# Loads of the normed activations h issued from ScalarE's queue instead of SP's

## Chip, cores and metric

The kernel runs on one core of a Trainium2 chip, in one launch. The metric is the device time of that launch in microseconds. Three runs of the kernel before gave 2426.85 us as median (2415.17 to 2428.43); one more execution was profiled.

## What is computed

One layer of a streaming encoder, for 2048 frames of a new stream (16 tiles of 128 rows) and for 8 running streams of 16 frames each (one more tile, called NT). The part that the change touches is the input projection:

```python
h = rms_norm(x, norm_g) * (1 + scale) + shift
qa, ka, va, za, qb, kb, vb, zb, ga, gb = split(h @ w_in)
```

`h` is (2176, 1024), `w_in` is (1024, 6144). Branch a is a differential softmax attention with rotated q and k (4 heads), branch b a stick-breaking attention (8 heads); each is gated with silu(z), goes through a matrix of its own, is weighted with sigmoid(g), and the sum goes through `w_out`, a residual and a last norm. Rotated keys and values are outputs too.

## The kernel before

Products need float32 accuracy, so each operand is kept as two float16 halves, high and low, and each product is three matmuls (high x high, high x low, low x high).

**Stage 1** (to about 140 us) makes h. It is written to DRAM, transposed and halved, as `hT_d`, one group of four tiles at a time (L1070). For the first unit h is still in the SBUF (`at_hand`).

**Stage 2** is one long interleaved stretch. There are 8 *units* u: four pairs of a head of branch a (`kind` 0) with two heads of branch b (`kind` 1). Within each unit the 17 tiles are worked off, NT first, then 0 to 15. `steps` lists the 136 pairs (u, t). For each:

- `fetch_h` (L400 to L403) loads h of the tile from `hT_d` into one of three SBUF buffers `hs`, taken in turn: 512 KB, one DMA on SP's queue. The buffer of load n is that of load n - 3.
- `project` (L405) gives 24 products of 512 columns (`mm`, L423 to L426: 8 pieces of the depth, three each) into a PSUM bank of the tag `mm`. `finish` then evacuates q, k, v and z (L440, L289, L452; for branch a the rotation on POOL, L459 to L464) and issues the stores (L474, L475, L477).
- `gate_piece` (L486 to L497) gives 24 products of 256 columns (512 in the last unit, none in the first) with the same h into the single bank of the tag `t`, evacuates them on ScalarE with L496, and stores them with L497. These are the last readers of the buffer.
- `transpose_qk` (L501) turns q and k on TensorE; `scores` (L614) gives the score products (L628 to L632), evacuated by L547 on VectorE (branch a) or as sigmoids by L119 on ScalarE (branch b), with the scan L605 behind them. Weights are split in halves (L289, L561, L562) and transposed by a DMA on SP's queue into `wt` (`turn`, L569); two steps later `pv` multiplies them with v (L676 to L681).

`line` (L839 to L869) is the list of the projection pieces of all steps in order, 12 pieces of two products each and then the gate pieces. At piece `H_AT` = 2 of step m it fetches h of step m + 1 (L855). For each step the main loop (L1202) takes as many pieces as are due and interleaves them with the score chunks and the value products by cost (`interleave`, L91). Preparation of the next unit's weights and norms of later operands (L828, one 512 KB load each) are spread between them.

That is the order in which the program is written. The framework then schedules it: it takes the instructions by their dependencies and by a modelled time, sets each into the queue of its engine, and adds the semaphore waits. An engine's queue is worked off in order. `tc.add_manual_dep` with `NOSYNC` adds an edge for the scheduler alone, without a semaphore; `act` (L117) uses it to keep the activations in order of writing. Each DMA counts up one of eight completion counters, given out in turn, and waits for the DMA that had its counter before.

**Stage 3** (from about 1797 us) applies the gates, the branch matrices and `w_out`, with the attention of the running streams beside it.

The functions that the change touches, and what calls them:

Of the kernel before, what the change touches and what calls it, by code (L numbers as in the profile page):

```python
# [23 lines left out]
NOSYNC = mybir.DependencyInfo(mybir.DependencyClass.NoSync, mybir.DependencyReason.DATA)  # L24
# [3 lines left out]
KT = D // P  # L28
# [81 lines left out]
def layer_kernel(ctx: ExitStack, tc: tile.TileContext, a: dict):  # L110
    nc = tc.nc
    V, S, G, T = nc.vector, nc.scalar, nc.gpsimd, nc.tensor
    load = nc.sync.dma_start
# [3 lines left out]
    def act(**kw):  # L117

        i = S.activation(**kw)  # L119
        if last_table[0] is not None:  # L120
            tc.add_manual_dep(i.ins, last_table[0].ins.name, NOSYNC, reason="table order")
        last_table[0] = i
        return i

    x_p = a["x_prompt"][0]
    x_s = a["x_sample"].rearrange("b s d -> (b s) d")
# [35 lines left out]
    hT_d = [dram.tile([P, w // P, 2, KT, P], F16, name=f"hT_d{g}") for g, (_, w) in enumerate(GROUPS)]  # L162
# [235 lines left out]
    at_hand, ahead, fetched = {}, {}, []  # L398

    def fetch_h(u, t):  # L400
        ahead[u, t] = hs[len(fetched) % 3].bitcast(F16).rearrange("p (f k n) -> p f k n", f=2, n=P)
        fetched.append(t)
        load(out=ahead[u, t], in_=hT_d[t // 4][:, t % 4, :, :, :])  # L403

    def project(U, t):  # L405

        kind, h, sc, sq = U["kind"], U["h"], U["sc"], U["sq"]
        g, i = t // 4, t % 4
        box = {}

        def start():
            if t in at_hand:
                box["h"] = at_hand.pop(t)
            else:
                if (U["u"], t) not in ahead:
                    fetch_h(U["u"], t)
                box["h"] = ahead.pop((U["u"], t))
            box["p"] = bank("mm")
            if kind == 0:
                box["r"] = stg.tile([P, 96], F32, tag="rope", name="rope")  # L420
                load(out=box["r"], in_=a["shapes"][:, t * 96 : t * 96 + 96])

        def mm(n):  # L423
            hi, wi = ((0, 0), (0, 1), (1, 0))[n % 3]
            k = n // 3
            T.matmul(box["p"], box["h"][:, hi, k, :], U["w"][k][:, wi, :], start=(n == 0), stop=(n == 3 * KT - 1))  # L426

        def piece(n):
            if n == 0:
                start()  # L430
            for j in range(2 * n, 2 * n + 2):
                mm(j)
            if n == 11:
                finish()
# [103 lines left out]
    def evacuate(job, seg, c, p, lo, n, sc_pos, sc_neg, ch):  # L538

        buffers(job, seg)  # L540
        if job["U"]["kind"] == 0:
            if "mx" not in job:
                job["mx"] = tiny.tile([P, 2, 4], F32, tag="mx", name="mx")
                job["nch"] = 0
            job["nch"] = max(job["nch"], ch + 1)
            dst = seg[("p", "n")[c]]
            V.tensor_scalar(out=dst[:, lo : lo + n], in0=p[:, 0:n], scalar1=sc_pos, scalar2=None,  # L547
                            op0=ALU.mult, op1=ALU.max, accum_out=job["mx"][:, c, ch : ch + 1])
        else:

            act(out=seg["p"][:, lo : lo + n], in_=p[:, 0:n], func=AF.Sigmoid, scale=sc_pos)
            act(out=p[:, 0:n], in_=p[:, 0:n], func=AF.Sigmoid, scale=sc_neg)
# [18 lines left out]
    def softmax_pair(job):  # L571

        segs = job["segs"]
        nm = tiny.tile([P, 2], F32, tag="nm", name="nm")
        V.tensor_reduce(out=nm, in_=job["mx"][:, :, 0 : job["nch"]], axis=AX.X, op=ALU.max, negate=True)
        l = tiny.tile([P, 2, 2], F32, tag="l", name="l")
        for i, seg in enumerate(segs):
            nk = (seg["hi"] - seg["lo"]) * P
            for c in range(2):
                w = seg[("p", "n")[c]][:, 0:nk]  # L580
                act(out=w, in_=w, func=AF.Exp, bias=nm[:, c : c + 1], accum_out=l[:, c, i : i + 1])
        r = tiny.tile([P, 3], F32, tag="r", name="r")
        sums = l[:, :, 0]
        if len(segs) > 1:
            V.tensor_tensor(out=sums, in0=l[:, :, 0], in1=l[:, :, 1], op=ALU.add)
        V.reciprocal(out=r[:, 0:2], in_=sums)
        V.scalar_tensor_tensor(out=r[:, 2:3], in0=sums[:, 0:1], scalar=r[:, 1:2], in1=nlam, op0=ALU.mult, op1=ALU.mult)
        V.tensor_tensor(out=r[:, 0:1], in0=r[:, 0:1], in1=ls[:, 0:1], op=ALU.mult)
        for seg in segs:
            nk = (seg["hi"] - seg["lo"]) * P  # L590
            p, n = seg["p"][:, 0:nk], seg["n"][:, 0:nk]
            V.scalar_tensor_tensor(out=p, in0=n, scalar=r[:, 2:3], in1=p, op0=ALU.mult, op1=ALU.add)
            turn(job, seg, r[:, 0:1])
# [253 lines left out]
    def projection(m):  # L847
        u, t = steps[m]
        made = []

        def piece(i):
            if i == 0:
                begin(u, t)
                made.extend(project(units[u], t))
            if i == H_AT and not at_hand and m + 1 < len(steps):  # L855
                fetch_h(*steps[m + 1])
            made[i]()

        return [lambda i=i: piece(i) for i in range(12 + 3 * GATES[u][1] // 128)]
# [342 lines left out]
    for n in range(len(steps) + PV_LAG):  # L1202
        made, qk, vs = [], [], []
        if n < len(steps):
            u, t = steps[n]
# [182 lines left out]
```

## Time and profile before

| | |
|---|---|
| three runs, median (lowest to highest) | 2426.85 us (2415.17 to 2428.43) |
| the profiled execution | 2416.58 us, span 2414.4 us |
| mean granted TensorE clock | 0.954 |
| stretch in which the loads of h are issued | 140 to 1797 us |
| DMAs on the one hardware queue | 75.3% of the DMA engines' time |

An engine's busy time leaves out the issuing of DMAs. In rows of waits, the line named waited for what stands behind the arrow: microseconds in total, how often, the longest. In the timeline a row is start, duration, engine, line, operation, tiles, count and, in brackets, how long the engine was idle just before. PEld is the weight load of TensorE, which runs ahead of the matmuls (PE): a stall for h shows first at PEld. SPq is SP's queue of DMA issues; ACTq is what ScalarE's sequencer does itself. Lines are those of the kernel before.

### The profile page before, as it was taken

What the parts mean: (1) busy time and instruction counts of PE and PEld (TensorE: products, weight loads), DVE (VectorE), ACT (ScalarE), POOL (GpSimd) and SP (SyncE); (2) the same over time, 40 slices, a digit from 0 to 9 for tenths busy, and PEclk for the clock granted to TensorE, in tenths of its full rate; (3) what the DMA queues carried; (4) which work ended last, traced back from release to release, by engine and by line L of the source; (5) the groups of instructions that cost most, each with busy time, mean ns of one, the idle gap of its engine ahead of it and who ended that gap; (6) DMA issues with size and microseconds to landing.
All of it is one profiled execution on the core that took longest, in us unless ns stands there. A gap on an engine that the chain in (4) does not pass through costs nothing. (4 is left out here: it accounts for less than half of the span.)

```text
span 2414.4 us, 45136 instructions
## 1 busy us (share of the span) xinstructions
PE 2129.1 (88%) x16366; PEld 1247.2 (52%) x16366; DVE 1746.9 (72%) x3668; ACT 1664.5 (69%) x3264; POOL 754.2 (31%) x607
## 2 busy tenths in 40 slices
PE   5879998899999899899988898999995688888998
PEld 2435665565665556556555555655553344444443
DVE  4868778886676788667778976657778767777754
ACT  3658788886777878566777876665777667666652
POOL 1733023453102346220124542102334333332322
PEclk7989999999999999999999999999997889999999
DMA  9668969985886998577588866756688999998521
GB/s 334 215 204 205 215 161 217 221 182 134 189 219 168 211 195 177 129 174 177 134 215 175 182 154 149 186 129 158 154 179 184 274 240 254 252 244 214 158 104 53
DMA packets 854000, 453.91 MB, mean 188 GB/s; under 512 B 539050, under 2 KB 806362, under 8 KB 853264
## 3 DMA queue, kind: packets, MB, share of 16 engines
q1 hardware_dynamic: 853776, 451.03, 75.3%
q8 instruction: 128, 2.10, 0.4%
q14 instruction: 96, 0.79, 0.1%
HBM read 249.80 MB, written 73.44 MB: 134 GB/s over the span
## 5 line engine op out<-in xcount | busy, mean ns | idle before, releaser
L611 POOL TENSOR_TENSOR sc_p<-sc_p,sc_n 128x127 f32<-128x127 f32 (+7 forms) x192 | 318.9, 1664 | 755.4 <-DVE sc_n L605 736.6
L426 PEld LDWEIGHTS <-hs 128*128 128x128 f16 x3120 | 278.9, 99 | 320.5 <-DMA hs<-hT_d 58.4
L426 PE MATMUL ps_mm<-wa,hs 128*128 128x512 f16 x1590 | 405.9, 388 | 28.3 <-DMA hs<-hT_d 28.3
L426 PE MATMUL ps_mm<-wb,hs 128*128 128x512 f16 x1530 | 391.2, 385 | 22.6 <-DMA hs<-hT_d 19.1
L493 PEld LDWEIGHTS <-hs 128*128 128x128 f16 x2856 | 275.5, 98 | 93.9 <-DVE qst L521 4.3
L605 DVE TENSOR_TENSOR_SCAN sc_n<-ps_s,sc_n,zero_t 128x512 f32<-128x512 f32 x192 | 245.6, 1279 | 48.6 <-ACT ps_s L119 42.4
L562 DVE TENSOR_TENSOR sc_n<-sc_p,sc_n 128x128 f16<-128x128 f32 (+7 forms) x192 | 232.1, 1214 | 27.8 <-ACT sc_n L561 27.3
L628 PE MATMUL ps_s<-k,qst 128*128 128x512 f16 (+3 forms) x640 | 224.8, 352 | 29.0 <-DVE sc_n L605 24.5
L493 PE MATMUL ps_t<-wb,hs 128*128 128x256 f16 (+1 forms) x1734 | 241.0, 292 | 0.7 <-DVE qst L521 0.6
L119 ACT ACTIVATE sc_p<-ps_s,usc 128x512 f32<-128x512 f32 (+3 forms) x320 | 206.1, 644 | 36.1 <-PE ps_s L629 17.8
L629 PE MATMUL ps_s<-k,qst 128*128 128x512 f16 (+3 forms) x640 | 224.1, 352 | 0.0
L119 ACT ACTIVATE ps_s<-ps_s,usc 128x512 f32<-128x512 f32 (+3 forms) x328 | 201.4, 614 | 0.0
L561 ACT CAST sc_n<-sc_p 128x128 f16<-128x128 f32 (+7 forms) x192 | 156.1, 818 | 64.3 <-POOL sc_p L611 63.9
L680 PE MATMUL ps_o<-v,wt 128*128 128x128 f16 x1088 | 156.7, 226 | 41.0 <-DMA wt<-sc_n 40.7
L1309 PE MATMUL ps_o<-wo,wb 128*128 128x512 f16 x816 | 188.9, 385 | 0.7 <-ACT wb L1127 0.7
L1268 PE MATMUL ps_mm<-wa,wb 128*128 128x512 f16 x612 | 166.4, 403 | 20.5 <-DVE sy L225 14.2
L459 POOL TENSOR_TENSOR rot<-pr,rope 128x256 f32<-128x256 f32 x68 | 62.5, 919 | 381.6 <-ACT pr L440 299.3
L547 DVE TENSOR_SCALAR_CACHE_REDUCE sc_p<-ps_s,usc 128x512 f32<-128x512 f32 (+3 forms) x160 | 106.6, 666 | 82.0 <-PE ps_s L629 58.7
L680 PEld LDWEIGHTS <-wt 128*128 128x128 f16 x1088 | 104.5, 102 | 93.3 <-DMA wt<-sc_n 53.2
L493 PE MATMUL ps_t<-wa,hs 128*128 128x256 f16 (+1 forms) x1122 | 148.7, 282 | 1.5 <-DVE qst L521 1.5
L547 DVE TENSOR_SCALAR_CACHE_REDUCE sc_n<-ps_s,usc 128x512 f32<-128x512 f32 (+3 forms) x160 | 106.6, 666 | 53.6 <-PE ps_s L629 28.4
L681 PE MATMUL ps_o<-v,wt 128*128 128x64 f16 x1088 | 144.8, 198 | 0.0
(338 smaller groups left out, 4530.7 us busy)
## 6 DMA issues: line engine op xcount, KB each, us to landing
hs<-hT_d SPq DMA_DIRECT2D x130, 512.0 KB, 4.3
wb<-g_d SPq DMA_DIRECT2D x26, 512.0 KB, 5.1
out_dram<-pr SPq DMA_DIRECT2D x204, 64.0 KB, 2.3
g_d<-gt SPq DMA_DIRECT2D x102, 128.0 KB, 3.8
wide<-in_w_ada_dram SPq DMA_DIRECT2D x12, 1024.0 KB, 8.9
wa<-in_w_in_dram SPq DMA_DIRECT2D x34, 256.0 KB, 6.2
z_d<-pr SPq DMA_DIRECT2D x136, 64.0 KB, 1.7
o_d<-o SPq DMA_DIRECT2D x136, 64.0 KB, 3.0
```

The costliest lines, as they stand in the source:

```text
L119: i = S.activation(**kw)
L426: T.matmul(box["p"], box["h"][:, hi, k, :], U["w"][k][:, wi, :], start=(n == 0), stop=(n == 3 * KT - 1))
L493: T.matmul(box["g"][:, 0:gw], box["h"][:, hi, k, :], U["wg"][k // per][:, k % per, wi, :], start=(j == 0), stop=(j == 3 * KT - 1))
L547: V.tensor_scalar(out=dst[:, lo : lo + n], in0=p[:, 0:n], scalar1=sc_pos, scalar2=None, op0=ALU.mult, op1=ALU.max, accum_out=job["mx"][:, ...
L562: V.tensor_tensor(out=lo, in0=src, in1=hi, op=ALU.subtract)
L605: V.tensor_tensor_scan(out=dst[:, lo : lo + n][:, ::-1], data0=src[:, 0:n][:, ::-1], data1=zero_t[:, 0:1].to_broadcast([P, n]), initial=fi ...
L611: G.tensor_tensor(out=p[:, 0:m], in0=p[:, 0:m], in1=n[:, 1 : m + 1], op=ALU.mult)
L628: T.matmul(p[:, 0:n], qst[:, c, :], kk[:, c, 0:n], start=True, stop=False)
L629: T.matmul(p[:, 0:n], qst[:, 2 + c, :], kk[:, c, 0:n], start=False, stop=not diag)
L680: T.matmul(po[:, c * P : (c + 1) * P], wt[:, wj, :], vt[:, c, :, :], start=first, stop=False)
L1268: T.matmul(pb, st["u"][:, ui * 8 + br * 4 + k, :], wb[br * 4 + k // 2 * 2 + j][:, wi, k % 2, :], start=(n == 0), stop=(n == 11))
L1309: T.matmul(po, st["y"][:, yi * 8 + k, :], wo[j * 4 + k // 2][:, wi, k % 2, :], start=(n == 0), stop=(n == 3 * KT - 1))
```

## The change

The load in `fetch_h` is issued by ScalarE (`nc.scalar.dma_start`) instead of SP. A helper `not_ahead` ties each load, by an edge for the scheduler alone, to the last projection product that has been written so far, so that the scheduler doesn't place it ahead of that product. `mm` keeps this product in `last_mm`.

```diff
+    last_mm = [None]
+
+    def not_ahead(i):
+
+        if last_mm[0] is not None:
+            tc.add_manual_dep(i.ins, last_mm[0].ins.name, NOSYNC, reason="place in the queue")
+
...
     def fetch_h(u, t):
         ahead[u, t] = hs[len(fetched) % 3].bitcast(F16).rearrange("p (f k n) -> p f k n", f=2, n=P)
         fetched.append(t)
-        load(out=ahead[u, t], in_=hT_d[t // 4][:, t % 4, :, :, :])
+        not_ahead(nc.scalar.dma_start(out=ahead[u, t], in_=hT_d[t // 4][:, t % 4, :, :, :]))
...
-            T.matmul(box["p"], box["h"][:, hi, k, :], U["w"][k][:, wi, :], start=(n == 0), stop=(n == 3 * KT - 1))
+            last_mm[0] = T.matmul(box["p"], box["h"][:, hi, k, :], U["w"][k][:, wi, :], start=(n == 0), stop=(n == 3 * KT - 1))
```

The lines behind the helper stand 7 lower in the changed kernel (L403 is L410 there). Nothing else is edited; since the scheduler places everything anew, other instructions change places too.

## The prediction

> **What bounds the kernel now.** I read the page first, then busy time by stretches, then the waits of TensorE and of SP's queue in the stretch where the loads stand, then the loads one by one on the timeline.
>
> ```profile
> span 2414.4 us, 45136 instructions
> PE 2129.1 (88%) x16366; PEld 1247.2 (52%) x16366; DVE 1746.9 (72%) x3668; ACT 1664.5 (69%) x3264; POOL 754.2 (31%) x607
> hs<-hT_d SPq DMA_DIRECT2D x130, 512.0 KB, 4.3
> 140.00:1797.00 1657.00, 1527.35 (x11784) 934.01 (x11783) 1221.03 (x2505) 1210.12 (x2550) 489.13 (x403) 0.98 0.76 179
> ```
>
> The last row is the stretch in which all 130 loads of h are issued: length, then busy time of PE, weight loads, DVE, ACT, POOL, then clock, DMA share and GB/s. TensorE is busy for 1527 of 1657 us, ACT for 73%. TensorE's queue bounds this stretch, so the change can be worth at most the 130 us in which TensorE is idle. Which waits are they?
>
> ```profile
> PEld L426 <- DMA hs<-hT_d: 58.4, 30, 7.4
> PEld L676 <- DMA wt<-sc_n: 34.7, 26, 3.7
> PEld L680 <- DMA wt<-sc_n: 32.2, 25, 3.2
> PE ps_mm L426 <- DMA hs<-hT_d: 47.4, 26, 7.0
> SPq L403 <- PE ps_t L493: 74.7, 32, 7.8
> L403 SPq DMA_DIRECT2D hs<-hT_d x130: 319/382/2542, 139.7 to 1759.0; - x130
> DMA to landing us min/median/max: 3.8/4.3/6.5
> ```
>
> The first and the fourth row are the same stalls, seen by weight loads and by matmuls: some 54 us, in 30 of 130 tiles, for h that has not landed. The next two are 67 us for transposed weights `wt`. The fifth says that SP stands 75 us at these loads, because the buffer is still being read. A load takes 0.38 us to issue and 4.3 us to land.
>
> Two tiles show two kinds of late load (start, duration, engine, line):
>
> ```profile
> 1026.93 0.97 PEld L493 LDWEIGHTS <-hs 128*128 128x128 f16 x9
> 1028.24 0.38 SPq L403 DMA_DIRECT2D hs<-hT_d  x1
> 1033.05 0.98 PEld L426 LDWEIGHTS <-hs 128*128 128x128 f16 x6 [2.99 <-DMA hs<-hT_d]
> ```
>
> ```profile
> 1262.25 6.64 SPq L569 DMA_TRANSPOSE wt<-sc_n  x2
> 1263.85 0.97 PEld L493 LDWEIGHTS <-hs 128*128 128x128 f16 x8
> 1267.67 0.52 ACT L496 ACTIVATE gt<-ps_t,usc 128x256 f32<-128x256 f32 x1
> 1268.94 1.02 SPq L477 DMA_DIRECT2D z_d<-pr  x1
> 1270.06 0.40 SPq L403 DMA_DIRECT2D hs<-hT_d  x1
> 1275.30 0.76 PEld L426 LDWEIGHTS <-hs 128*128 128x128 f16 x5 [2.80 <-DMA hs<-hT_d]
> ```
>
> In the first, the last gate product on the buffer (L493) ends near 1028.2, the load goes out at once, and TensorE still waits 2.99 us: **bound by the buffer**. In the second the buffer is free near 1265 and the load leaves at 1270, because SP was issuing two transposes until 1268.9: **bound by SP's queue**. Going so through the 30 stalls, from
>
> ```profile
> 331.36 0.38 SPq L403 DMA_DIRECT2D hs<-hT_d  x1
> 337.31 0.34 PEld L426 LDWEIGHTS <-hs 128*128 128x128 f16 x3 [3.12 <-issue]
> ...
> 1554.97 0.53 SPq L403 DMA_DIRECT2D hs<-hT_d  x1
> 1560.11 0.11 PEld L426 LDWEIGHTS <-hs 128*128 128x128 f16 x2 [0.95 <-DMA hs<-hT_d]
> ```
>
> (the first and the last), 12 us would remain had each load left when its buffer was free and landed in 4.3 us, 22 us with 5.0 us. The other 32 to 42 us are SP's lateness and long landings.
>
> **The change, part by part.** *Where the loads go.* The built order puts 77 of the 130 directly behind L496, the evacuation of the gate product that reads the buffer last; the rest stand behind other evacuations, most of them with plenty of time. None waits for TensorE any more: L496 has waited for it just before. So a tight load still can't leave before the gate product ends, and the 12 to 22 us stay. The order on TensorE changes too. I added up TensorE's work between a buffer's last gate product and the first product of the tile loaded into it, at the rates of these rows, 0.21 us a projection product and 0.11 us a gate product:
>
> ```profile
> 616.64 4.66 PEld L426 LDWEIGHTS <-hs 128*128 128x128 f16 x23
> 647.53 2.71 PEld L493 LDWEIGHTS <-hs 128*128 128x128 f16 x24
> ```
>
> This room is under 5 us (issue and landing) for 14 loads before and 22 after; what they lack sums to 18 and 30 us. The gates have moved back, towards the tile that needs the buffer: +12 us.
>
> *Lateness of the new queue.* In place of SP's queue the load passes ScalarE's:
>
> ```profile
> L496 ACT ACTIVATE gt<-ps_t,usc x119: 452/474/709, 266.9 to 1797.5; 128x256 f32<-128x256 f32 x102, 128x512 f32<-128x512 f32 x17
> L496 ACTq EVENT_SEMAPHORE  x104: 17/17/221, 276.2 to 1796.5; - x104
> PE ps_t L493: 60.4, 36
> ```
>
> In 36 of 119 cases ACT itself waited for the gate, so the load behind it is punctual; in the rest L496 starts later, as at 1267.67, over 2 us behind its gate product. The second row says that ScalarE's sequencer is ahead of its engine: its last semaphore wait for L496 is at 1796.5, the instruction itself at 1797.5. A load, which the sequencer issues, can thus go out up to a microsecond ahead of what stands before it, but not ahead of their waits. Its lateness lies between none (-36 us) and that of a queue with many waits of its own (+20 us); I take SP's, less 2 us in all. With the +12 us, **h waits: +10 us**, ends -36 and +32.
>
> The Trainium skill (Perfetto Trace Analysis, DVE / Act Engine Instruction) says that the sequencer pushes an instruction into a wait queue and decodes the next; the rows just read agree.
>
> *New waits.* 124 loads wait for completion counts of one or two earlier DMAs, 107 of them for one that SP issues. Mostly these have landed long ago. Where they haven't, ScalarE stands:
>
> ```profile
> 1654.08 2.54 SPq L569 DMA_TRANSPOSE wt<-sc_n  x2
> 1656.53 0.71 ACT L496 ACTIVATE gt<-ps_t,usc 128x512 f32<-128x512 f32 x1
> L569 SPq DMA_TRANSPOSE wt<-sc_n x273: 1167/1622/6136, 158.9 to 1796.5; - x137
> DVE sc_n L605 <- ACT ps_s L119: 78.8, 90, 4.0
> PE ps_s L628 <- DVE sc_n L605: 14.2, 18, 2.6
> ```
>
> The load behind this L496 waits for the first of the two transposes: issued at 1654.08, landed some 4.3 us later, near 1658.4, so it stands 1.8 us. By such times of before, 6 loads would stand for 10 us together, and 19 for 33 us were SP 2 us later. Behind the load stand most often (45 of 130) the sigmoids of L119; the scan L605 waits for them, and the scores L628 for the scan (last two rows), whose 14 us show how seldom that reaches TensorE.
>
> *Issue on ScalarE.* 130 x 0.38 = 50 us at most. Cover is L496 itself, 0.47 us on the engine while the sequencer issues; without cover all 50 us would be added to an engine busy at 73%. Issue and standing together: nothing to 83 us; I take **+6 us**, near the lower end, since the sequencer runs ahead.
>
> *SP relieved.* It loses 50 us of issues and the 75 us of waits. SP's issues in the stretch are 273 transposes at 1.62 us and, by the order, 990 others at about 0.38 us, some 820 us; 50 us is 6% of these, 125 us 15%. Of the 67 us for `wt` that makes 4 to 10 us; I take **-6 us**, ends 0 and -20. It is not more, since SP mostly waits for a transpose's data, not the data for SP:
>
> ```profile
> SPq L569 <- DVE sc_n L562: 68.2, 34, 8.2
> SPq L569 <- DVE sc_n L547: 45.3, 14, 10.0
> ```
>
> Computation, bytes and everything after 1797 us are as before: nothing. **Sum: +10 + 6 - 6 = +10 us.** The profiled execution took 2416.58 us (span 2414.4 and 2.2 around it): 2426.6, so 2427 us. The median of the runs shown is 2426.85 (2415.17 to 2428.43), so the profiled execution is a low one; on the median the sum would be 2437.
>
> **The rivals.**
> *SP's lateness simply goes* (faster). For: the second example, where L496 starts 2.4 us before SP issues the load. Against: the room after has shrunk, and a slow queue is replaced by a busy one. 32 to 42 us, say 37, and 6 us of `wt`: 2374 us.
>
> *A queue of their own* (faster). Stalled loads took up to 6.5 us to land, the quickest 3.8. If in their own queue they no longer trail SP's transfers and land in 3.8 us, the 30 stalls lose at most 29 us: 2427 - 29 = 2398 us. Against: DMA share is 0.76, and the transfers that they overtake include `wt`.
> The Trainium skill (DMA: Bandwidth & Descriptors, Queues, rings and completion order) has each DMA engine take turns between the rows of SP and ACT, which is this case; its section Issuing engines are not separate DMA queues says that only issue time is saved, by which this rival's 29 us would not come. No run here shows either.
>
> *Transposes hold both queues* (slower). If descriptors for a transpose keep ScalarE's load waiting as they keep SP's, the load gains nothing, and ScalarE stands as long. 273 x 1.62 = 443 us is 27% of the stretch, so 35 of the 130 loads meet one and stand for half of 1.62 us, 28 us, or for up to 6 us each. It decides where the standing exceeds ScalarE's lead of about 1 us: then the evacuations behind are late too. 10 us of h, 28 us of standing and as much again in h that lands later, less 20 us that the lead hides: +46, 2463 us. Against: the engine has idle time.
> The Trainium skill (Perfetto Trace Analysis, DMA Instruction — HWDGE (DVE, Sync)) says that an issuing sequencer locks one shared descriptor generator; by that rule this rival holds. Before has one queue and can't show it.
>
> *The change doesn't do what it says*: the loads stand behind the gate's evacuation, the gates move back, and lateness stays as it was with the new waits on top: +20 us, 2437 us (slower).
>
> **How the numbers follow.** Forecast (within 2411 to 2439 us) 0.40; SP's lateness goes 0.14; queue of their own 0.08; transposes hold both 0.24; not what it says 0.14. About 0.5% (12 us) is what a measurement can tell from no change: faster 0.22, same 0.40, slower 0.38. The range 2390 to 2465 us takes in the second rival, the fourth and most of the third; it leaves out the first (0.14) and the third's far end.
>
> **What would show it.** Right: in after, PEld's wait for `hs` stays at 50 to 75 us, and tight loads follow L496 closely. Wrong to the fast side: that wait falls under 30 us with loads landing near 3.8 us. Wrong to the slow side: load issues on ACT of over 1 us in number, or ACT waiting in front of them. SP's relief: waits for `wt` under 67 us. The forecast fails, whatever the h wait does, if the changed order makes TensorE wait for other tiles.

## The result, and the profile after

The changed kernel takes 2463.36 us (median, 2460.99 to 2471.22), the kernel before beside it 2426.10 us (2415.17 to 2428.43). The ratio is 1.0166, 95% interval 1.0133 to 1.02: slower by some 37 us, beyond the forecast's 2411 to 2439 us. It still lies in the wide range of 2390 to 2465 us, near the time of a rival, and whether that is more than luck is looked at below. The profiled execution took 2460.99 us, its span is 2459.2 us, 44.8 us above that of before (the profiled execution of before, 2416.58 us, was a quick one).

First the new queue and the load's own rows in the profile of the changed kernel (lines behind the helper stand 7 higher than before):

```profile
q10 hardware_dynamic: 18720, 68.17, 9.7%
...
L410 ACTq DMA_DIRECT2D hs<-hT_d x130: 325/326/391, 146.4 to 1806.4; - x130
DMA to landing us min/median/max: 3.6/4.4/7.8
```

The loads have a hardware queue of their own now (q10). Issuing one takes 0.33 us, 0.39 at most. Where the trace has a landing (22 of the 130), it comes after 4.4 us in the median; before it was 4.3. Nothing here is slow, so the load itself is not the loss. The stretch to the last evacuation of a gate, before and after (length, then busy time of PE, PEld, DVE, ACT, POOL, then clock, DMA share, GB/s), and the stretch behind it:

```profile
140.00:1798.20 1658.20, 1528.55 (x11804) 934.97 (x11803) 1221.82 (x2506) 1211.32 (x2553) 489.13 (x403) 0.98 0.76 179
1798.20:2414.40 616.20, 509.73 (x3999) 263.56 (x3995) 433.77 (x922) 381.79 (x578) 197.55 (x128) 0.91 0.76 198
```

```profile
140.00:1842.50 1702.50, 1544.40 (x11805) 944.16 (x11805) 1216.10 (x2510) 1210.23 (x2553) 481.69 (x404) 0.97 0.76 174
1842.50:2459.20 616.70, 505.44 (x3999) 262.17 (x3995) 437.30 (x922) 381.20 (x578) 197.20 (x128) 0.92 0.77 198
```

All of the loss, 44.3 us, lies in the stretch of the loads; the rest takes 616 us in both. It has two parts. TensorE stands idle for 158.1 us in place of 129.7 (length less busy time): +28.4. And the same products keep it busy for 15.9 us longer, at a clock of 0.97 in place of 0.98. Which waits grew, in the changed kernel:

```profile
PEld L683 <- DMA wt<-sc_n: 51.2, 32, 8.5
PEld L687 <- DMA wt<-sc_n: 43.5, 27, 10.0
PEld L433 <- DMA hs<-hT_d: 33.0, 18, 8.1
PE ps_s L635 <- DVE sc_n L612: 30.5, 28, 4.6
...
SPq L504 <- ACT gt L503: 99.9, 44, 7.1
```

Against the rows in the prediction: the wait for h fell (at PEld from 58.4 to 33.0 us, 30 tiles to 18), but the wait for the transposed weights `wt` rose from 66.9 to 94.7, and that for the scan at the matmuls from 14.2 to 30.5. SP, which was to be relieved, stands 99.9 us at the gate's store (15.3 before): it waits for the same gates one instruction later.

### The profile page after: what moved, and what is told of

Its sections match the earlier page's. It is cut to its first block, busy times and chain, and to the rows that moved or that the text cites. A ratio compares the mean times of both kernels' runs of the same rounds, so it can differ in the third digit from the quotient of the medians.

```text
span 2459.2 us, 45004 instructions
## 1 busy us (share of the span) xinstructions
PE 2138.6 (87%) x16366; PEld 1254.3 (51%) x16366; DVE 1743.8 (71%) x3668; ACT 1662.8 (68%) x3264; POOL 745.9 (30%) x607
## 5 line engine op out<-in xcount | busy, mean ns | idle before, releaser
L433 PE MATMUL ps_mm<-wa,hs 128*128 128x512 f16 x1590 | 406.9, 390 | 16.8 <-DMA hs<-hT_d 16.3
L635 PE MATMUL ps_s<-k,qst 128*128 128x512 f16 (+3 forms) x640 | 227.2, 356 | 44.5 <-DVE sc_n L612 38.9
L569 DVE TENSOR_TENSOR sc_n<-sc_p,sc_n 128x128 f16<-128x128 f32 (+7 forms) x192 | 224.5, 1174 | 38.3 <-ACT sc_n L568 37.8
L636 PE MATMUL ps_s<-k,qst 128*128 128x512 f16 (+3 forms) x640 | 227.5, 358 | 0.0
```

Source lines behind the costliest of these rows:

```text
L433: last_mm[0] = T.matmul(box["p"], box["h"][:, hi, k, :], U["w"][k][:, wi, :], start=(n == 0), stop=(n == 3 * KT - 1))
L569: V.tensor_tensor(out=lo, in0=src, in1=hi, op=ALU.subtract)
L635: T.matmul(p[:, 0:n], qst[:, c, :], kk[:, c, 0:n], start=True, stop=False)
L636: T.matmul(p[:, 0:n], qst[:, 2 + c, :], kk[:, c, 0:n], start=False, stop=not diag)
```

## The experiments

Two things changed at once, the queue and the scheduler's order of everything else: between the two kernels, of TensorE's 32,200 instructions alone some 9,500 stand in another place. So the first task was to change one without the other. In eight kernels the program is built twice. From the first build the order of every engine's queue is read off; in the second each instruction is tied to its predecessor in that order, by an edge for the scheduler alone:

```diff
+    def pin(tc, traced, order):
...
+        for engine, name in order:
+            i = by.get(name)
+            if i is None or i.engine != engine:
+                continue
+            if engine in last:
+                tc.add_manual_dep(i, last[engine], NOSYNC, reason="pinned")
+            last[engine] = name
...
+    _, _, order = build(ORDER_OF, None)
+    nc, arrays, done = build(RUN_WAY, order)
```

Everything but the moved DMAs then stands exactly as in the kernel whose order is taken; the same technique serves in all experiments below with "order of".

**Queue against order.** *p1_old_order_act* takes the order of before and puts the loads on ScalarE; *p2_new_order_sp* takes the order of the changed kernel and leaves them on SP.

```diff
p1:    +ORDER_OF = "sp"
       +RUN_WAY = "act_tied"
p2:    +ORDER_OF = "act_tied"
       +RUN_WAY = "sp"
```

> All instructions of every engine stand in the order of the kernel before; only the 130 loads of h leave SP's queue and stand in ScalarE's (79 of them directly behind the gate's evacuation). Theory ORDER (the scheduler's new order of everything else costs the 37 us, the queue does not): the time of before, 2426 us within 10, or a little less if SP is relieved. Theory QUEUE (a load on ScalarE's queue, or what it does to SP's queue and to the transposed weights, costs the 37 us): 2455 to 2470 us, with the waits for wt risen as in the changed kernel (from 67 to about 95 us at the weight loads).

> All instructions of every engine stand in the order of the changed kernel; only the 130 loads of h are taken back to SP's queue. Theory ORDER: the time of after, 2463 us within 10, with the waits for wt as high as there; or more, if ScalarE's queue had helped: the wait for h fell from 58 to 33 us, so up to 25 us more. Theory QUEUE: 2426 us within 10.

| | loads on SP | loads on ScalarE |
|---|---|---|
| order of before | 2422.22 us | 2438.85 us, ratio 1.0061 (1.0038 to 1.0085) |
| order of the changed kernel | 2438.53 us, ratio 1.0079 (1.0054 to 1.0104) | 2463.36 us, ratio 1.0166 (1.0133 to 1.02) |

Neither theory holds alone: each half costs some 16 us, and together they make 1.40% (0.61% and 0.79%) of the 1.66%; the rest is within the intervals. Only the queue differs between before and p1. First the two rows of before that the prediction doesn't show, then p1 (lines 17 higher):

```profile
PE ps_o L676 <- DMA wt<-sc_n: 25.0, 20, 3.6
PE ps_o L680 <- DMA wt<-sc_n: 24.5, 21, 2.9
```

```profile
140.00:1818.10 1678.10, 1536.30 (x11804) 942.85 (x11803) 1219.17 (x2506) 1211.65 (x2553) 490.77 (x403) 0.97 0.76 177
...
PEld L697 <- DMA wt<-sc_n: 49.2, 27, 5.9
PEld L693 <- DMA wt<-sc_n: 47.6, 31, 6.3
PE ps_o L697 <- DMA wt<-sc_n: 41.6, 24, 5.8
PE ps_o L693 <- DMA wt<-sc_n: 37.6, 27, 6.2
PEld L443 <- DMA hs<-hT_d: 28.1, 14, 9.5
PE ps_mm L443 <- DMA hs<-hT_d: 23.6, 13, 9.1
PE ps_s L645 <- DVE sc_n L622: 22.5, 19, 3.4
```

By the matmuls' rows, the queue takes 23.8 us from the wait for h and gives 29.7 to that for `wt` and 8.3 to that for the scan. The stretch is 19.9 us longer: idle +12.1, slower products +7.8. Why `wt`? Here is the tile of the prediction's second example again, first the wait for `wt` behind it in before, then the same tile in p1, with the load on ScalarE:

```profile
1271.37 0.10 PEld L680 LDWEIGHTS <-wt 128*128 128x128 f16 x1 [1.31 <-DMA wt<-sc_n]
```

```profile
1272.45 6.78 SPq L586 DMA_TRANSPOSE wt<-sc_n  x2
1277.15 0.33 ACTq L414 DMA_DIRECT2D hs<-hT_d  x1
...
1286.11 0.11 PEld L697 LDWEIGHTS <-wt 128*128 128x128 f16 x1 [5.93 <-DMA wt<-sc_n]
```

Before, the load left after the two transposes, 2.8 us too late for TensorE, and the second transpose landed in time for a stall of 1.3 us. Now the load leaves in the midst of them, 0.33 us to issue; its stall is gone, and TensorE waits 5.9 us for the second transpose. The load has overtaken that transpose, which lands 10.4 us after SP starts it (1275.65 to 1286.07); before it took 4.4 us (1266.96 to 1271.33).

To see whether that is the rule I took each transpose that TensorE waited for, from its (last) issue to the end of the wait, and set apart those with a load of h in flight for over 0.5 us of it (4.3 us of flight where the trace has no landing). With none in flight they take 4.7 us in before (44 of 63) and 4.7 in p1 (31 of 71). With one in flight they take 5.3 us in before (19), 6.0 in p1 (40), 6.5 in the changed kernel (39 of 72). Twice as many of these transposes meet a load, and on average those take over a microsecond longer. A long transpose also has more time in which to meet a load, so this count alone doesn't tell cause from effect; the loads of 128 KB below do. The transposes are not issued later: SP starts those that TensorE waits for 1.16 us behind their data in before, 1.11 in p1.

In p2 only the order differs from before (lines 17 higher):

```profile
140.00:1821.10 1681.10, 1541.57 (x11801) 942.45 (x11799) 1212.62 (x2503) 1212.64 (x2553) 480.72 (x403) 0.97 0.75 176
...
PEld L443 <- DMA hs<-hT_d: 68.0, 30, 6.1
PEld L697 <- DMA wt<-sc_n: 26.0, 23, 3.2
PEld L693 <- DMA wt<-sc_n: 24.3, 20, 3.8
PE ps_s L645 <- DVE sc_n L622: 20.3, 23, 2.6
PE ps_t L523 <- ACT gt L513: 10.1, 3, 6.0
```

The wait for h rises by 9.6 us (58.4 to 68.0), which fits the gates that moved back, though every other move of the order is in it too; the wait for `wt` falls (66.9 to 50.3). Idle time is 9.9 us above before, slower products make 13.0.

**The naive move, and the edge alone.** *e1_act_no_edge* drops `not_ahead` and keeps ScalarE's queue; *e2_sp_edge* keeps `not_ahead` around SP's load.

```diff
e1:    -        not_ahead(nc.scalar.dma_start(out=ahead[u, t], ...))
       +        nc.scalar.dma_start(out=ahead[u, t], ...)
e2:    -        not_ahead(nc.scalar.dma_start(out=ahead[u, t], ...))
       +        not_ahead(load(out=ahead[u, t], ...))
```

> The loads go to ScalarE's queue without the edge to the last projection product; the scheduler makes yet another order of everything (115 of 130 loads directly behind the gate's evacuation). Theory ORDER: a time of its own, anywhere between 2415 and 2475 us, going with the order and not with the queue. Theory QUEUE: 2455 to 2470 us as after, since the queue is the same.

> The edge alone: the loads stay in SP's queue and are tied to the last projection product; the scheduler makes yet another order (half as many products of TensorE change place as in the changed kernel). Theory ORDER: a time of its own between 2415 and 2475 us. Theory QUEUE: 2426 us within 10. If the edge is what costs: 2463 us.

e1 took 2463.28 us, ratio 1.0161 (1.013 to 1.0191), e2 2411.72 us, ratio 0.9956 (0.9935 to 0.9977). So the edge is not what costs: alone it gives the fastest full kernel so far. e1 fits QUEUE in its number, but its order is its own, so it doesn't separate the two; its wait for `wt` is the highest of all (109.8 us at PEld), for h 26.5.

**What about the queue costs: the bytes beside the transposes, or the issue?** Both kernels have the order of before and loads of 128 KB; only the queue differs between them. They leave out three quarters of h: the products (those of the gate likewise, not shown) read the loaded quarter in its place, so the work is the same and the values are others.

```diff
-            T.matmul(box["p"], box["h"][:, hi, k, :], ...)
+            T.matmul(box["p"], box["h"][:, hi % HALVES, k % DEPTH, :], ...)
...
-        load(out=ahead[u, t], in_=hT_d[t // 4][:, t % 4, :, :, :])
+        load(out=ahead[u, t][:, 0:HALVES, 0:DEPTH, :], in_=hT_d[t // 4][:, t % 4, 0:HALVES, 0:DEPTH, :])
```

> The order of the kernel before on every engine, the loads on ScalarE's queue as in p1_old_order_act, but each load brings only a quarter of h (128 KB: the high half, four of eight depths), and the products read that quarter in place of the rest; so the sums are of other data, the work of every engine is the same. Theory BESIDE (a load in a queue of its own runs beside the transposes of the weights and makes them land later: in p1_old_order_act the waited-for transposes took 6.0 us from issue with a load in flight, 4.7 us without): with a quarter of the bytes the queue costs nothing any more; within 6 us of q_sp_small or below it, with waits for wt at most 10 us above those there. Theory ISSUE (what costs is the issue and the standing on ScalarE's queue, 130 x 0.33 us and what stands behind it): still 12 to 20 us above q_sp_small.

> The same quarter loads in the order of the kernel before, on SP's queue as before. The waits for h fall, since the load lands earlier: 2390 to 2415 us by either theory. It is the base for q_act_small: theory BESIDE has the two within 6 us, theory ISSUE has q_act_small 12 to 20 us slower.

q_act_small took 2393.53 us (ratio 0.9866, 0.9848 to 0.9883), q_sp_small 2390.73 (0.9855, 0.9838 to 0.9872): 2.8 us apart, where the full loads were 17 apart. The stretch and the waits on ScalarE's queue, then on SP's (lines 18 higher than before):

```profile
140.00:1774.70 1634.70, 1529.32 (x11807) 941.90 (x11807) 1220.99 (x2511) 1209.41 (x2553) 491.04 (x404) 0.98 0.67 150
...
PEld L694 <- DMA wt<-sc_n: 36.2, 29, 5.0
PEld L698 <- DMA wt<-sc_n: 31.0, 22, 4.4
PE ps_mm L444 <- DMA hs<-hT_d: 9.8, 5, 7.4
```

```profile
140.00:1769.70 1629.70, 1529.41 (x11802) 940.36 (x11801) 1218.95 (x2503) 1207.87 (x2553) 488.05 (x403) 0.98 0.66 151
...
PEld L694 <- DMA wt<-sc_n: 31.5, 23, 3.7
PEld L698 <- DMA wt<-sc_n: 30.5, 22, 5.2
PE ps_mm L444 <- DMA hs<-hT_d: 17.0, 10, 5.0
```

With a quarter of the bytes the move to ScalarE's queue raises the wait for `wt` by 5.2 us (62.0 to 67.2), in place of 29.9 (66.9 to 96.8). Nearly as many of the waited-for transposes meet a load as in p1 (33 of 64), but these take 5.0 us, the others 4.6. So the rise of `wt` goes with the bytes: for it, BESIDE holds.

The 2.8 us are not the whole price of issue, standing and the new completion waits, which are the same 130 instructions here, because the wait for h falls too: by the matmuls' rows from 17.0 to 9.8 us. TensorE's idle time grows by 5.1 us all the same (100.3 to 105.4). Beside h (-7.2) and `wt` (+2.6), some 10 us thus come from other waits: 3.3 from that for the scan, 3.5 from that for the evacuation of q, the rest in small pieces. In p1 the same remainder is 6 us (12.1 + 23.8 - 29.7). What makes it, the issue on ScalarE or something else, is not shown.

**Is it SP's standing at the gate's store?** SP's longest wait in the changed kernel invites that. *g_store_act* (order of before) sends the gate's store to ScalarE as well:

```diff
-                load(out=g_d[t][:, g0 : g0 + gw], in_=gt[:, 0:gw])
+                nc.scalar.dma_start(out=g_d[t][:, g0 : g0 + gw], in_=gt[:, 0:gw])
```

> The order of the kernel before on every engine; the loads of h on ScalarE's queue as in p1_old_order_act, and the stores of the gate on it too, so that SP no longer stands 81 us for the gate's evacuation. Theory STANDING (the transposes are late because SP stands at the gate's store): the waits for wt fall back to 70 us and the time to 2415 to 2425 us. Theory BESIDE: SP's standing is not what makes them late, the stores too now run beside the transposes: 2430 to 2450 us, waits for wt near 100 us.

2452.89 us, ratio 1.011 (1.009 to 1.013), by the ratios some 12 us above p1 and 3 us over the range that BESIDE gave. SP no longer stands there, and the waits for `wt` are no lower than the 96.8 us of p1 (lines 17 higher):

```profile
PEld L693 <- DMA wt<-sc_n: 54.7, 34, 6.9
PEld L697 <- DMA wt<-sc_n: 45.3, 28, 4.4
```

STANDING falls; the longest wait on SP's queue was not a cost. What makes this kernel slower than p1 is hardly these waits (+3.2 us), and stays open.

**Only the late loads.** If 130 loads beside the transposes cost 30 us of `wt`, and only some 19 gain by leaving SP, those should go alone. *few_old_order* does so in the order of before with 19 loads (shown), *few_edge_order* in that of e2 with 18, where every load keeps `not_ahead`.

```diff
-        load(out=ahead[u, t], ...)
+            if len(fetched) - 1 in LATE:
+                not_ahead(nc.scalar.dma_start(out=ahead[u, t], ...))
+            else:
+                load(out=ahead[u, t], ...)
```

> The order of the kernel before on every engine; only the 19 loads for which TensorE waited in its trace and which left SP over 1.2 us after their buffer was free go to ScalarE's queue (each directly behind the gate's evacuation); 111 stay on SP. Theory BESIDE: the lateness of those 19 goes as in p1_old_order_act (waits for h from 58 to 30-40 us), and only 19 loads run beside transposes instead of 130, so the waits for wt rise by some 5 us instead of 36: 2400 to 2415 us, faster than before. Rival, PER LOAD (every tight load that leaves early takes from a transpose what it gains, so choosing loads helps nothing): 2420 to 2440 us.

> The order of e2_sp_edge on every engine (2411.7 us with all loads on SP), with 18 loads of the same kind on ScalarE's queue. Theory BESIDE: 5 to 20 us under e2_sp_edge, 2392 to 2407 us. Rival PER LOAD: 2411 to 2425 us.

2417.70 us, ratio 0.9979 (0.9965 to 0.9993), and 2408.46 us, ratio 0.994 (0.9919 to 0.996). Both lie between the two theories. Waits of few_old_order (the products' lines stand 23 higher than before):

```profile
PEld L703 <- DMA wt<-sc_n: 40.6, 29, 3.8
PEld L699 <- DMA wt<-sc_n: 36.3, 30, 3.5
PEld L449 <- DMA hs<-hT_d: 26.6, 17, 7.3
PE ps_s L651 <- DVE sc_n L628: 26.0, 24, 3.3
```

The 19 loads bring the whole gain of h (58.4 to 26.6 us, as with 130). But they cost 10.0 us of `wt` (66.9 to 76.9), half a microsecond each, where 130 cost 29.9, 0.23 each. A likely reason, argued and not tested: SP was late with just these loads because it was issuing transposes, so these are the loads that meet transposes when they leave on time. The wait for the scan also rose, from 14.2 to 26.0; its cause stays open. Against e2 the 18 loads bring 3 us, which the two intervals don't tell apart.

**A third order, and the spread of orders.** *p3_edge_order_act* is the order of e2 with all loads on ScalarE; *o_fetch_at_3* is the kernel before with one constant changed.

```diff
p3:    +ORDER_OF = "sp_tied"
       +RUN_WAY = "act_tied"
o:     -H_AT = 2
       +H_AT = 3
```

> The order of e2_sp_edge on every engine, with all 130 loads on ScalarE's queue: a third order in which only the queue differs. The queue cost 17 us in the order of before and 25 us in that of the changed kernel. Theory BESIDE: 15 to 27 us above e2_sp_edge, 2427 to 2439 us, waits for wt near 100 us, for h near 30 us. If the queue's cost hung on those two orders: no change against 2411.7 us.

> The kernel before, loads on SP, with H_AT = 3 instead of 2: the loads are written one piece later, and the scheduler makes another order of everything. It shows how far the time goes with the order alone, beside 2411.7 (e2_sp_edge), 2422 (before) and 2438.5 us (p2_new_order_sp). Theory ORDER (the order moves the time by up to some 20 us either way): 2400 to 2445 us. If the order of before is special: over 2445 us.

p3 took 2425.50 us (ratio 1.0012, 0.9995 to 1.003), 14 above e2 and 1.5 short of the range that BESIDE gave, with waits of 92.3 us for `wt` and 25.8 for h at PEld. So the queue costs 0.56%, 0.61% and 0.86% in three orders (quotients of the ratios). o_fetch_at_3 took 2422.04 us (ratio 1.0005, 0.9987 to 1.0023). With all loads on SP, four orders thus lie between 0.9956 and 1.0079 of before: the scheduler's order moves the time as much as the queue does, in either direction.

## Why the prediction was wrong

**The step that failed first is *SP relieved*: "I take -6 us".** It was worked out from SP's time alone: fewer issues, so earlier transposes. p1 shows +29.9 us (66.9 to 96.8 at PEld), the changed kernel +27.8. The transposes did leave as early as before; what changed is what flies beside them. On one queue, as in the second example, SP's lateness had been keeping loads behind the transposes. The prediction had this in half a sentence, against the rival *a queue of their own* ("the transfers that they overtake include `wt`"), and gave it no price.

**"I take SP's, less 2 us in all"**, on the lateness of the new queue, was wrong as well, to the other side: p1 shows -30.3 us at PEld (58.4 to 28.1), near the end of -36 that was named. With it the h wait came to -25.4 us in the changed kernel, where the sum had +10. (Its lower end, -36, left the gates' +12 out; with them it is -24.) The rival *SP's lateness simply goes* was right about h, and right only there.

**"With the +12 us"** for the gates that moved back was near: p2, with the whole order changed, shows +9.6.

**"Issue and standing together: ... I take +6 us"** can't be told apart from the rest: what is left of TensorE's idle time beside h and `wt` is 6 us in p1 and 10 us in the pair with small loads. But the 14 us of the wait for the scan, read there as a sign of how seldom a late sigmoid reaches TensorE, came to 30.5 us in the changed kernel (22.5 in p1, 20.3 in p2). This rise of 16.3 us had no term in the sum, and its cause stays open.

**"Computation ... as before: nothing"** is the second term that failed: it missed 15.9 us of the 44.3. The products are the same but the granted clock isn't. From the changed kernel, stretches of 2 us around a stall for `wt` (clock third from the end):

```profile
408.00:410.00 2.00, 0.00 (x0) 0.00 (x0) 0.00 (x0) 1.02 (x2) 0.48 (x1) 0.96 1.14 108
410.00:412.00 2.00, 0.00 (x0) 0.00 (x0) 0.00 (x0) 0.00 (x0) 0.00 (x0) 0.50 1.26 106
...
414.00:416.00 2.00, 1.51 (x19) 1.51 (x20) 0.00 (x0) 0.00 (x0) 0.00 (x0) 0.50 1.03 231
416.00:418.00 2.00, 2.00 (x10) 0.99 (x9) 1.34 (x5) 0.52 (x1) 0.02 (x1) 0.50 0.49 154
418.00:420.00 2.00, 2.00 (x6) 0.75 (x5) 1.79 (x3) 2.00 (x6) 0.39 (x1) 0.50 0.34 96
420.00:422.00 2.00, 2.00 (x11) 0.88 (x9) 2.00 (x3) 1.55 (x4) 1.06 (x1) 0.98 0.88 230
```

TensorE stands for 9.5 us, in the midst of which the clock is halved, and then works on at half clock for over 5 us (from 414.5 to 420). So this stall is paid for again afterwards. Added up over the stretch from each trace's granted clock, work at half clock costs (half of the time in which TensorE works at 0.50) 25.5 us in before, 35.0 in p1, 41.1 in p2 and 40.4 in the changed kernel; without it the products take 1503, 1501, 1501 and 1504 us, so to within some 3 us the clock accounts for the slower products. The medians of the mean clock over all runs agree: 0.954, 0.947, 0.949 and 0.946. Stalls of TensorE of over 4 us are 2, 3, 5 and 6. The sum of waits was the wrong measure; their lengths count too. The Trainium skill (TensorE: Matmul & The Clock Gate, HAM oscillation — how this bites in real kernels) warns of gaps of TensorE above some 3.4 us, because the clock then falls to half. The rows of this stall agree.

**The order** stood in the prediction as a condition of failure only ("the forecast fails ... if the changed order makes TensorE wait for other tiles") and as +12 us of h. On SP's queue the changed order is worth 16 us (p2); beside h, TensorE waits 6.5 us more for the gate's evacuation (3.6 us in before, 10.1 at L523) and the clock 13.0.

**The rivals.** *Transposes hold both queues* named 2463 us, which is what came, but by a mechanism that the trace excludes; that the number fits is luck. In the changed kernel 35 of the 130 loads, as many as the rival counted, were issued wholly within the time in which SP was issuing a transpose. None of the 130 took over 0.39 us, and the semaphore instructions ahead of them took 17 ns each. The sections of the Trainium skill cited in the prediction part here as well. The shared descriptor generator of the Trainium skill (Perfetto Trace Analysis, DMA Instruction — HWDGE (DVE, Sync)) would have held such a load until SP was done. The same 0.39 us speak against it. The Trainium skill (DMA: Bandwidth & Descriptors, Queues, rings and completion order) also has each DMA engine take turns between the rows of the queues. This fits p1, where the load goes through beside transposes issued ahead of it. *The change doesn't do what it says* (2437 us) is refuted by the wait for h.

Among the complete kernels three beat before: few_edge_order (0.994), e2_sp_edge (0.9956) and, barely, few_old_order (0.9979, 0.9965 to 0.9993).

## What to carry to other kernels

A transfer that gets a queue of its own doesn't only stop waiting; here it ran beside what it used to follow. Before you move one, list what it will overlap, and ask whether TensorE is waiting for that too: here 30 us of waits for h became 30 us of waits for the transposed weights, and more time at half clock. And where a scheduler places everything anew, hold its order fixed before you credit or blame an edit: here the order alone was worth -11 to +16 us.

## What the runs showed that I had not expected

Short stalls also cost clock. In the kernel before, the first example of the prediction (2.82 us without a product, at 1030 to 1033 us) is followed by this, in stretches of 2 us:

```profile
1032.00:1034.00 2.00, 0.94 (x5) 0.47 (x6) 0.58 (x3) 1.95 (x4) 0.00 (x0) 1.00 0.70 210
1034.00:1036.00 2.00, 2.00 (x7) 0.64 (x5) 1.58 (x4) 0.26 (x3) 0.00 (x0) 0.50 1.08 299
1036.00:1038.00 2.00, 2.00 (x8) 0.81 (x7) 0.00 (x0) 1.04 (x1) 0.00 (x0) 0.65 0.25 61
```

TensorE is at work again and loses 1.7 us to the halved clock (2 x 0.50 + 2 x 0.35). Between 300 and 1500 us the same trace has 13 such drops, each behind a stall of 2.0 to 4.1 us; 16 stalls there are that long. So the 3.4 us of the Trainium skill (TensorE: Matmul & The Clock Gate, HAM oscillation — how this bites in real kernels) is not where it begins here.
